# Feed-forward hidden tiles of a hybrid layer made in seven block products in place of eight, with halved weights and weight sums on GpSimd

## The chip, the core and the metric

One core of a Trainium2 chip runs the whole program. The time is device microseconds of one execution of that core. The five engines work beside each other, each through its own instructions in order: TensorE (PE, with its weight loads PEld), VectorE (DVE), ScalarE (ACT), GpSimd (POOL) and SyncE (SP, which here only issues transfers). They wait for each other by semaphores.

## What is computed

One layer over 1056 tokens (1024 of a prompt, 32 of a second group) of 1024 features, in float32. `c` gives nine modulation rows; each of three steps is modulated, gated and normed:

```python
mod = (silu(c) @ w_ada + b_ada)                # 9 rows of 1024, for each of two groups
f = swiglu(modulate(x, 0), w1, w3, w2)         # silu(h @ w1) * (h @ w3), then @ w2; 2816 hidden
x = layer_norm(ALPHA * x + 0.5 * gate(0) * f)
m = mix(modulate(x, 1))                        # gated linear recurrence and spatial gating
x = layer_norm(ALPHA * x + gate(1) * m)
f = swiglu(modulate(x, 2), ...)                # second feed-forward, own weights
x = layer_norm(ALPHA * x + 0.5 * gate(2) * f)
```

The change concerns `h @ w1` and `h @ w3` of both feed-forwards.

## The kernel before

**Layout.** Activations lie feature-major: a feature tile of 128 rows by the tokens, in three chunks of 384, 384 and 288 tokens (`CH`). A hidden tile is 128 of the 2816 hidden features; there are 22 in each feed-forward.

**Products.** Float32 numbers are kept as two parts of fp32r, a high and a low one (`split`, line 176: ScalarE copies the high part at L177, VectorE subtracts it from the source at L178, GpSimd does so in a few places of the start and the mixing). A product is three passes, high x high, high x low and low x high (`h_mm`, all through `mm`, L132). Each matmul has one weight load of its own.

**A hidden tile** (`H`, from L639): for w1 and then w3, eight contraction tiles by three chunks by three passes, into three PSUM banks. ScalarE makes silu of the first (L659), VectorE multiplies it with the second out of PSUM (L666), and the result is split into `g`. The banks come from eight that everything shares.

**An F pass** (`F`, from L745) multiplies the hidden tiles of a block with their w2, for eight output tiles m and three chunks; `add_gated` (L713) adds gate x product to the running sum `xa` (first feed-forward) or `xb` (second). Blocks are nine pairs, [18] and [19, 20, 21]; `ffn_order` lets one further hidden tile run ahead of each pass. The first three hidden tiles are made in special loops (`ffn_first`, `H_chunks`), the last block in `last_f`, chunk by chunk with the norm behind it.

**Weights** come in 512 KB raw tiles (four buffers, by SP's transfers `raw<-wst`) in the order of `stream_order`, and are split into five buffers `whl` of 128 x 2 x 1024. `w_rel` splits the next as one is used up.

**The modulation.** Rows 0 and 1 are made at the start on TensorE. Rows 2 to 8 are made beside the first feed-forward in `ada_rest` (from L576): each in two halves of 512, as 16 products of a raw tile with a number per partition on VectorE (L601, L603, accumulator `acc`), split (`acchl`), summed over partitions by TensorE (`psm`), copied out by ScalarE (L620) to `row`, written to HBM by a GpSimd transfer (L622, `mrow`) and read back turned by two more (L625); VectorE adds the bias (L627, `mod`). Row 2 is the gate `gt` of the first feed-forward, so its first gated addition needs it.

**Order.** TensorE's instructions stand in program order. Those of VectorE, ScalarE and GpSimd are ordered by a scheduler within the program; `ada_rest` is a side program that is taken up as TensorE's work passes by (`yield` gives microseconds of it).

Of the kernel before, what the change touches and what calls it, by code (L numbers as in the profile page):

```python
# [29 lines left out]
# token chunks; the last one ends with the 32 sample tokens  # L30
# [4 lines left out]
# columns of the packed per-feature vectors  # L35
# [10 lines left out]
# row-parallel blocks of the feed-forward's hidden tiles  # L46
BLOCKS = [[2 * b, 2 * b + 1] for b in range(9)] + [[18], [19, 20, 21]]
# [25 lines left out]
def ffn_order():  # L73
    """Program of one feed-forward: ('H', t) and ('F', block), in order."""
    o = [("H", 0), ("H", 1)]
    nxt = 2
    for b in BLOCKS[:-1]:
        o.append(("H", nxt))
        nxt += 1
        o.append(("F", b))  # L80
        if len(b) == 2 and nxt < 19:
            o.append(("H", nxt))
            nxt += 1
    while nxt < FF:
        o.append(("H", nxt))
        nxt += 1
    o.append(("F", BLOCKS[-1]))
    return o


def stream_order():
    s = []
    for n in (1, 2):
        for kind, a in ffn_order():
            if kind == "H":
                s += [(f"f{n}w1", a), (f"f{n}w3", a)]
            else:
                s += [(f"f{n}w2", t) for t in a]
        if n == 1:
            s += [("ga", j) for j in range(4)] + [("xa", j) for j in range(3)]  # L100
            s += [("vs", j) for j in range(4)] + [("xa", 3)] + [("us", j) for j in range(4)]
            s += [("wo", j) for j in range(8)]
    return s


class Tot:
    """A sum over feature tiles: the first `direct` ones go to TensorE alone, VectorE adds the others up in t."""


class Core:  # L110
    def __init__(self, tc, ins, outs):
        self.tc, self.nc = tc, tc.nc
        self.i, self.o = ins, outs
        self.pe = 0.0
        self.side = []
        self.ntot = 2
        self.mods = set()
        self.window = False
        self.ln_out = {}

# [14 lines left out]
    def go(self, gen, kind=None):  # L135
        """Run a side program beside the main one; it yields the time it has to wait."""
# [15 lines left out]
    def drain(self, e, out=False):  # L152
        """Finish a side program, or a norm up to its output; earlier norms first."""
# [7 lines left out]
    def w_init(self):  # L161
        self.order = stream_order()
        self.raws = {}
        self.ws = {}
        self.n_raw = self.n_split = self.n_rel = self.n_get = 0

    def w_raw(self):
        n = self.n_raw
        if n >= len(self.order):
            return  # L170
        r = self.wpool.tile([P, 1024], F32, tag="raw", name="raw", bufs=4)
        self.nc.sync.dma_start(r, self.i["wst"][n])
        self.raws[n] = r
# [5 lines left out]

    def w_split(self, e=None):  # L180
        n = self.n_split
        e = e or (self.nc.gpsimd if self.window else None)
        if n >= len(self.order):
            return
        while self.n_raw <= n:
            self.w_raw()
        w = self.wpool.tile([P, 2, 1024], F32R, tag="whl", name="whl", bufs=5)
        r = self.raws.pop(n)
        self.split(w[:, 0, :], w[:, 1, :], r, e)
# [3 lines left out]
    def w_get(self, what):  # L193
        n = self.n_get
# [14 lines left out]
    def run(self):  # L209
# [4 lines left out]
        # pools over PSUM have eight one-bank buffers  # L214
# [38 lines left out]
        with tc.manual_schedule(engines={E.DVE, E.Activation, E.Pool}):  # L253
# [38 lines left out]
    def startup(self):  # L292
# [29 lines left out]
        # silu(c) in its two parts: [feature, k, (part, group)]  # L322
# [24 lines left out]
        def turn(i):  # L347
            """Rows i, turned, into two banks of four feature tiles."""
# [1002 lines left out]
```

## Time and profile before

| | |
|---|---|
| runs, median of 3 | 1986.9 us (1986.7 to 1988.58) |
| the profiled execution's span | 1981.3 us; 5.6 us of the median lie around it |
| start and the first three hidden tiles | up to 137.9 us |
| first feed-forward, 200 to 600 us | PE busy 400.0 of 400, VectorE 260.2, ScalarE 78.2, GpSimd 20.5 |
| end of the first feed-forward and mixing, 800 to 1200 us | PE busy 387.7 of 400, VectorE 271.1, clock 0.97 |
| second feed-forward, 1200 to 1800 us | PE busy 600.0 of 600, VectorE 227.5, ScalarE 115.3, GpSimd 0.9 |
| DMA | 70 GB/s over the span |

The page gives busy time and share of the span for each engine; a group's row has line, engine, operation, tiles, shapes and count, then the busy time in us and the mean of one in ns, then the idle time just ahead and what ended it. A window's row has start and end, length, and the busy time (with counts) of the engines. A row of the timeline has start, length, engine, line and operation. Waits of the present:

```
engine line waited for: us in total, times, longest us
DVE mod L627 <- DMA mod<-mrow: 26.7, 13, 4.5
POOL mod L625 <- DMA mrow<-row: 45.7, 14, 4.0
ACT g L177 <- DVE s L666: 318.0, 38, 12.5
```

### The profile page before, as it was taken

The numbers are of one execution on the slowest core, as the hardware profiler recorded it, in microseconds if no ns is written. First come the engines' busy times: TensorE is split into PE (matmuls) and PEld (weight loads), VectorE is DVE, ScalarE is ACT, GpSimd is POOL, SyncE is SP. The second block draws the span as 40 slices with busy tenths as digits, with TensorE's granted clock in tenths as the row PEclk, the third lists the DMA queues.
The fourth block names the chain that finished last, engine by engine and source line by source line (L and its number), as shares of the span: only waits on it lengthen the run. The fifth ranks groups of instructions, "written<-read, shape, count | busy, mean of one in ns | idle before, by whom it ended". The sixth has DMA issues, their size and how long they took to land.

```text
span 1981.3 us, 27961 instructions
## 1 busy us (share of the span) xinstructions
PE 1931.3 (97%) x11818; PEld 1886.5 (95%) x11818; DVE 1096.0 (55%) x1988; ACT 540.8 (27%) x848; POOL 90.4 (5%) x102
## 2 busy tenths in 40 slices
PE   7999999999999999989999999999999999999996
PEld 4899999999999999989889999999999999999996
DVE  8885765765664344763977375432442343244457
ACT  6542121212112111244544347111111111111114
POOL 2100000000000000022000000000000000000000
PEclk9999999999999999989899999999999999999998
DMA  7333223222322111121012311111111111110102
GB/s 281 130 126 101 95 84 117 97 75 96 102 95 71 54 43 44 54 80 67 14 59 67 130 36 40 54 43 54 43 34 63 43 43 44 54 43 33 33 1 88
DMA packets 40429, 140.13 MB, mean 71 GB/s; under 512 B 5588, under 2 KB 8276, under 8 KB 39536
## 3 DMA queue, kind: packets, MB, share of 16 engines
q1 hardware_dynamic: 37040, 128.98, 18.8%
q10 hardware_dynamic: 1920, 9.24, 1.2%
q0 software_dynamic: 1344, 0.12, 0.4%
q8 instruction: 93, 1.52, 0.3%
q14 instruction: 32, 0.26, 0.0%
HBM read 129.53 MB, written 8.79 MB: 70 GB/s over the span
## 4 chain that ended last, share of the span: by engine, by line
PE 78%; issue 10%; DVE 7%; ACT 2%; DMA 2%; POOL 0%; SPq 0%; POOLq 0%; DVEq 0%; ACTq 0%
PE ps L132 74%; PE psl L132 1%; DVE xl L462 1%; DVE acc L603 1%; PE psm L132 1%; PE psa L132 1%; DMA mod<-mrow 1%; PE psg L132 1%; DVE tot L719 0%; DMA mrow<-row 0%; ACT t L452 0%; DMA raw<-ada 0%; DVE xa L713 0%; DVE xb L832 0%; DVE t L843 0%
## 5 line engine op out<-in xcount | busy, mean ns | idle before, releaser
L132 PE MATMUL ps<-xh,whl 128*128 128x384 f32 (+1 forms) x5184 | 1245.4, 324 | 2.4 <-ACT xh L459 1.9
L132 PEld LDWEIGHTS ps<-xh,whl 128*128 128x128 f32 x5184 | 910.5, 189 | 7.0 <-ACT xh L459 2.1
L132 PE MATMUL ps<-xl,whl 128*128 128x384 f32 (+1 forms) x2592 | 839.3, 324 | 4.2 <-DVE xl L462 4.2
L132 PE MATMUL ps<-g,whl 128*128 128x384 f32 (+1 forms) x3168 | 522.2, 325 | 1.8 <-DVE xa L713 1.3
L132 PEld LDWEIGHTS ps<-g,whl 128*128 128x128 f32 x3168 | 513.2, 189 | 6.8 <-DVE xa L713 1.9
L132 PEld LDWEIGHTS ps<-xl,whl 128*128 128x128 f32 x2592 | 488.2, 188 | 7.7 <-DVE xl L462 6.0
L178 DVE TENSOR_TENSOR whl<-raw,whl 128x1024 fp32r<-128x1024 f32 x145 | 176.9, 1232 | 265.2 <-ACT whl L177 265.1
L177 ACT ACTIVATE whl<-raw 128x1024 fp32r<-128x1024 f32 x156 | 164.3, 1056 | 361.0 <-PE ps L132 356.6
L713 DVE SCALAR_TENSOR_TENSOR xb<-ps,gt,xb 128x384 f32<-128x384 f32 (+2 forms) x384 | 165.2, 486 | 109.6 <-PE ps L132 95.3
L666 DVE TENSOR_TENSOR s<-s,ps 128x384 f32<-128x384 f32 (+1 forms) x117 | 56.1, 520 | 246.9 <-PE ps L132 246.9
L603 DVE SCALAR_TENSOR_TENSOR acc<-raw,cs,acc 128x512 f32<-128x512 f32 x196 | 137.4, 747 | 56.9 <-DMA raw<-ada 56.9
L713 DVE SCALAR_TENSOR_TENSOR xa<-ps,gt,xa 128x256 f32<-128x256 f32 (+1 forms) x352 | 149.6, 487 | 17.1 <-PE ps L132 16.7
L177 ACT ACTIVATE g<-s 128x384 fp32r<-128x384 f32 x132 | 60.6, 488 | 342.7 <-DVE s L666 318.0
L659 ACT ACTIVATE s<-ps 128x384 f32<-128x384 f32 (+1 forms) x114 | 51.1, 457 | 277.2 <-PE ps L132 276.6
L178 DVE TENSOR_TENSOR g<-s,g 128x384 fp32r<-128x384 f32 x132 | 65.2, 519 | 3.8 <-ACT g L177 3.8
L476 POOL TENSOR_TENSOR r<-r,half 128x3 f32<-128x3 f32 x8 | 7.4, 920 | 1143.2 <-DVE r L475 1143.2
L462 DVE TENSOR_TENSOR xl<-t,xh 128x384 fp32r<-128x384 f32 (+3 forms) x48 | 42.4, 886 | 17.2 <-ACT xh L459 16.4
L132 PE MATMUL ps<-whl,xh 128*128 128x512 f32 (+1 forms) x144 | 46.4, 404 | 0.0
L177 ACT ACTIVATE acchl<-acc 128x512 fp32r<-128x512 f32 x28 | 17.7, 633 | 97.4 <-DVE acc L603 88.6
L452 ACT ACTIVATE t<-xa,AB 128x384 f32<-128x384 f32 (+1 forms) x64 | 34.1, 596 | 34.6 <-DVE AB L506 20.0
L132 PEld LDWEIGHTS ps<-whl,xh 128*128 128x128 f32 (+1 forms) x144 | 26.6, 187 | 7.1
L470 ACT ACTIVATE xb<-xb,aB,aG 128x384 f32<-128x384 f32 (+1 forms) x48 | 28.6, 669 | 14.3 <-DMA xb<-sp 14.3
(188 smaller groups left out, 899.8 us busy)
## 6 DMA issues: line engine op xcount, KB each, us to landing
raw<-wst SPq DMA_DIRECT2D x156, 512.0 KB, 3.2
raw<-ada SPq DMA_DIRECT2D x64, 512.0 KB, 3.3
wnat<-ada SPq DMA_DIRECT2D x4, 1024.0 KB, 13.0
xt<-x SPq DMA_DIRECT2D x7, 512.0 KB, 7.4
sp<-xa ACTq DMA_DIRECT2D x2, 1536.0 KB, 5.1
xb<-sp ACTq DMA_DIRECT2D x2, 1536.0 KB, 10.2
y<-xb SPq DMA_DIRECT2D x4, 768.0 KB, 3.2
sp<-xa ACTq DMA_DIRECT2D x1, 1152.0 KB, 4.1
```

Of the source, the lines that this page charges most:

```text
L132: self.nc.tensor.matmul(out, a, b, start=start, stop=stop, skip_group_check=True)
L177: self.nc.scalar.activation(dst_h, src, AF.Copy)
L178: (e or self.nc.vector).tensor_tensor(dst_l, src, dst_h.bitcast(F32), ALU.subtract)
L452: self.nc.scalar.activation(tmp[:, j, a:a + w], X[:, k, a:a + w], AF.Identity, scale=self.A[:, s, k, v:v + 1], bias=self.B[:, s, k, v:v + 1])
L462: V.tensor_tensor(xl, tmp, xh.bitcast(F32), ALU.subtract)
L470: return self.nc.scalar.activation(X[:, k, :], X[:, k, :], AF.Identity, scale=self.aG[:, s, k:k + 1], bias=self.aB[:, s, k:k + 1])
L476: self.nc.gpsimd.tensor_tensor(out, out, self.half[:n, :w], ALU.pow)
L603: V.scalar_tensor_tensor(acc[:, v, :], r[:, kk, :], self.cs[:, k, v:v + 1], acc[:, v, :], ALU.mult, ALU.add)
L659: self.nc.scalar.activation(s[:, :n], ps[c][:, :n], AF.Silu)
L666: self.nc.vector.tensor_tensor(s, s, ps[c][:, :n], ALU.mult)
L713: V.scalar_tensor_tensor(X[:, m, a + o:a + o + w], ps[:, o:o + w], self.gt[:, s, m, v:v + 1], X[:, m, a + o:a + o + w], ALU.mult, ALU.add)
```

## The change

For hidden tiles 3 to 21 of both feed-forwards (38 of 44), chunks 0 and 1 are computed by the Strassen-Winograd scheme. A tile's weights are seen as a 2 x 2 matrix of blocks: rows w1 and w3, columns the contraction's halves k 0-3 and 4-7 (A11, A12 for w1, A21, A22 for w3). The activations are B11, B21 (halves of chunk 0) and B12, B22 (of chunk 1). Then

S1 = A21 + A22, S2 = S1 - A11, S3 = A11 - A21, S4 = A12 - S2; T1 = B12 - B11, T3 = B22 - B12, T2 = T3 + B11, T4 = B21 - T2.

Seven products A11 B11, A12 B21, S4 B22, A22 T4, S1 T1, S2 T2, S3 T3 and some sums give the four results; eight were needed before. The T are made once in each feed-forward on VectorE (`combs`, `comb_last`; T2 takes B12's place), the S for each tile by four GpSimd sums out of the raw tiles (L238 to L243), and GpSimd also makes the low parts of these four (152). Chunk 2 is made as before, by the halves A11, A12, A21, A22 (`third`).

The core of the diff, the new tile (`H_fast`; `p_mm` is a block product of 4 contraction tiles x 3 passes):

```diff
+        self.p_mm(pa, a11, B11, True, False)
+        S.activation(s1, pa[:, :n], AF.Copy)
+        third(0, 0, a11)
...
+        self.p_mm(pb, s2, self.T2, True, False)
+        add(u2, s1, pb)
...
+        self.p_mm(pa, a12, B21, False, True)
+        sa = self.silu(0, pa)
+        third(0, 1, a12)
...
+        self.p_mm(pc, w, self.T1, True, False)
...
+        self.p_mm(pb, w, self.T3, False, True)
+        add(s1, s1, pb)
+        add(u4, s1, pc)
...
+        self.p_mm(pf, a22, self.T4, True, True)
+        add(s1, s1, pf)
+        self.glu_end(g, 0, sa, s1)
...
+        self.p_mm(pc, w, B22, False, True)
+        add(u2, u2, pc)
+        S.activation(u2, u2, AF.Silu)
+        self.glu_end(g, 1, u2, u4)
```

`add` is a VectorE sum out of PSUM (L838), `glu_end` the multiplication (L679) and the split. The sums of the weights:

```diff
+        if h == "S2":
+            x = self.wpool.tile([P, 1024], F32, tag="raw", name="wsum", bufs=RAWS)
+            G.tensor_tensor(x[:, 0:512], a["A21"], a["A22"], ALU.add)
+            G.tensor_tensor(x[:, 512:1024], x[:, 0:512], a["A11"], ALU.subtract)
+        if h == "S3":
+            G.tensor_tensor(a["A11"], a["A11"], a["A21"], ALU.subtract)
+        if h == "S4":
+            G.tensor_tensor(a["A12"], a["A12"], self.sums[nm, t][:, 512:1024], ALU.subtract)
```

Around it:

- Weights are split in halves of 512 columns into a ring of eight buffers `wh` of 128 x 2 x 512 (five of 1024 before), with a few homes elsewhere; there are five raw buffers (four before), which also hold the S.
- Blocks are [0, 1, 2], then pairs [3, 4] to [17, 18], then [19, 20, 21]; a block's F pass follows its last hidden tile directly, in two halves of w2.
- In `ada_rest` the accumulator has one buffer (two before), the split halves have a place of their own, and a half row goes out as two pieces of 256, by two transfers (L733), before the two that read it back (L736); the bias is added at L738, and the products are L715 and L717.
- The last tile's chunk 2 is made later, between products of its F pass.
- The start's natural weights come in 512 KB pieces; GpSimd's space for descriptors is 1024 bytes.

**Three places in the engines' orders.** First, VectorE in the modulation phase, near the seventh hidden tile. Before (waits for a semaphore in brackets; DMASW is a GpSimd transfer, DMAHW one of SP, names end in a running number):

```order
L666 TENSOR_TENSOR s_1012<-s_1012,ps_1018 128x384 [waits PE_49]
L603 SCALAR_TENSOR_TENSOR acc_1093<-raw_1094,cs_80,acc_1093 128x512 [waits DMAHW6_49,DVE_49]
L603 SCALAR_TENSOR_TENSOR acc_1093<-raw_1094,cs_80,acc_1093 128x512 [waits DVE_49] x3
L178 TENSOR_TENSOR whl_1136<-raw_882,whl_1136 128x1024 [waits DMAHW7_49,Activation_49]
L627 TENSOR_TENSOR mod_74<-mod_74,vec_68 128x8 [waits DMASW2_49,DMASW1_49]
L178 TENSOR_TENSOR g_901<-s_1012,g_901 128x384 [waits Activation_49]
L666 TENSOR_TENSOR s_1014<-s_1014,ps_1019 128x384
L666 TENSOR_TENSOR s_1016<-s_1016,ps_1020 128x288
L603 SCALAR_TENSOR_TENSOR acc_1093<-raw_1115,cs_80,acc_1093 128x512 [waits DMAHW7_49,DVE_49]
L178 TENSOR_TENSOR g_901<-s_1014,g_901 128x384 [waits Activation_49]
L178 TENSOR_TENSOR g_901<-s_1016,g_901 128x288 [waits Activation_49]
```

After:

```order
L738 TENSOR_TENSOR mod_74<-mod_74,vec_68 128x8 [waits DMASW7_49,DMASW6_49]
L717 SCALAR_TENSOR_TENSOR acc_3297<-raw_3368,cs_80,acc_3297 128x512 [waits DMAHW7_49,DVE_49]
L528 SCALAR_TENSOR_TENSOR AB_75<-mod_74,vec_68 128x16 [waits DVE_49]
L529 SCALAR_TENSOR_TENSOR AB_75<-mod_74,vec_68 128x16
L838 TENSOR_TENSOR s_3222<-s_3222,ps_3207 128x384 [waits PE_49]
L530 TENSOR_TENSOR AB_75<-AB_75,mod_74 128x16 [waits DVE_49]
L717 SCALAR_TENSOR_TENSOR acc_3297<-raw_3368,cs_80,acc_3297 128x512
L838 TENSOR_TENSOR s_3354<-s_3222,ps_3208 128x384 [waits DMASW5_49,DVE_49]
L717 SCALAR_TENSOR_TENSOR acc_3297<-raw_3368,cs_80,acc_3297 128x512
L838 TENSOR_TENSOR s_3222<-s_3222,ps_3209 128x384 [waits DVE_49,PE_49]
L717 SCALAR_TENSOR_TENSOR acc_3297<-raw_3368,cs_80,acc_3297 128x512
```

The bias addition to `mod`, which waits for two GpSimd transfers, now stands ahead of the block sums L838 of a tile (s1, u4, s1) with modulation products between them; before, it stood ahead of a split and two multiplications of a tile that was complete in PSUM.

Second, GpSimd at a half row of the modulation. Before, only the transfers:

```order
L622 DMA mrow4_1_2791<-row_2789 2x512 [waits DMASW7_49,Activation_49]
L625 DMA mod_74<-mrow4_1_2791 128x4x1 [waits DMASW7_49,DMASW0_49]
L625 DMA mod_74<-mrow4_1_2791 128x4x1
L622 DMA mrow5_0_3161<-row_3159 2x512 [waits DMASW2_49,Activation_49]
L625 DMA mod_74<-mrow5_0_3161 128x4x1 [waits DMASW3_49,DMASW2_49]
L625 DMA mod_74<-mrow5_0_3161 128x4x1
```

After:

```order
L238 TENSOR_TENSOR wsum_3262<-raw_3204 128x512 [waits DMAHW4_49,Pool_49]
L239 TENSOR_TENSOR wsum_3262<-wsum_3262,raw_3095 128x512 [waits DMAHW3_49,Pool_49]
L241 TENSOR_TENSOR raw_3095<-raw_3095,raw_3204 128x512 [waits DMAHW0_49,DVE_49,Pool_49]
L208 TENSOR_TENSOR wh_3261<-wsum_3262,wh_3261 128x512 [waits Activation_49]
L733 DMA mrow4_1_3282<-s_3283 2x256 [waits Activation_49]
L733 DMA mrow4_1_3282<-s_3286 2x256 [waits Activation_49]
L736 DMA mod_74<-mrow4_1_3282 128x4x1 [waits DMASW6_49,DMASW5_49,DMASW4_49]
L736 DMA mod_74<-mrow4_1_3282 128x4x1 [waits DMASW7_49]
L243 TENSOR_TENSOR raw_3095<-raw_3095,wsum_3262 128x512 [waits DVE_49]
L208 TENSOR_TENSOR wh_3338<-wsum_3262,wh_3338 128x512 [waits Activation_49]
```

The row's transfers now stand between sums and low parts of weights, and the sum S4 (L243) and the low parts behind them come after the wait for the first transfers.

Third, VectorE in the second feed-forward, from the end of one F pass into the next hidden tile. Before:

```order
L178 TENSOR_TENSOR whl_14011<-raw_13797,whl_14011 128x1024 [waits DMAHW3_49,Activation_49]
L178 TENSOR_TENSOR whl_14094<-raw_14014,whl_14094 128x1024 [waits DMAHW4_49,Activation_49]
L666 TENSOR_TENSOR s_14099<-s_14099,ps_14105 128x384 [waits PE_49]
L666 TENSOR_TENSOR s_14101<-s_14101,ps_14106 128x384 [waits DVE_49,PE_49]
L666 TENSOR_TENSOR s_14103<-s_14103,ps_14107 128x288 [waits PE_49,Activation_49]
L178 TENSOR_TENSOR g_14018<-s_14099,g_14018 128x384 [waits Activation_49]
L178 TENSOR_TENSOR whl_14180<-raw_14016,whl_14180 128x1024 [waits DMAHW5_49,Activation_49]
L178 TENSOR_TENSOR g_14018<-s_14101,g_14018 128x384 [waits Activation_49]
L178 TENSOR_TENSOR g_14018<-s_14103,g_14018 128x288 [waits Activation_49]
```

After, the second tile of a pair:

```order
L208 TENSOR_TENSOR wh_14203<-raw_14068,wh_14203 128x512 [waits Activation_49]
L838 TENSOR_TENSOR s_14121<-s_14121,ps_14106 128x384 [waits DVE_49,PE_49]
L208 TENSOR_TENSOR wh_14221<-raw_14139,wh_14221 128x512 [waits DMAHW6_49,Activation_49]
L838 TENSOR_TENSOR s_14219<-s_14121,ps_14107 128x384 [waits DVE_49]
L838 TENSOR_TENSOR s_14121<-s_14121,ps_14108 128x384 [waits DVE_49,PE_49]
L679 TENSOR_TENSOR s_14172<-s_14172,s_14121 128x384 [waits DVE_49]
L208 TENSOR_TENSOR g_14236<-s_14172,g_14236 128x384 [waits Activation_49]
L838 TENSOR_TENSOR s_14155<-s_14155,ps_14107 128x384 [waits PE_49]
L679 TENSOR_TENSOR s_14155<-s_14155,s_14219 128x384 [waits Activation_49]
L208 TENSOR_TENSOR wh_14292<-raw_14139,wh_14292 128x512 [waits Activation_49]
L208 TENSOR_TENSOR g_14236<-s_14155,g_14236 128x384 [waits Activation_49]
L679 TENSOR_TENSOR s_14186<-s_14186,ps_14264 128x288 [waits PE_49]
```

A tile's row of three multiplications became sums s1, u4, s1, a multiplication, the sum u2 and two more multiplications, each with its own wait, and a low part of a weight half (the tile `wh` ahead of u4) stands between the first two.

More of the change, by code (lines that the diff above doesn't have):

```diff
@@ L162, in w_init, with home @@
         self.order = stream_order()
+        self.raw_list = raw_order()
         self.raws = {}
         self.ws = {}
+        self.sums = {}
         self.n_raw = self.n_split = self.n_rel = self.n_get = 0
+        self.ring = [self.home(e) is None for e in self.order]
+    def home(self, e):
+        if e[:2] in (("xa", 0), ("xa", 3)):
+            return "mixr", "wx"
+        if e[:2] == ("f2w1", 2):
+            return "gpool", "tx"
+        if e[0] in ("f1w2", "f2w2") and e[1] in BLOCKS[-1] and e[2] == 1:
+            return "gpool", "tx"
+        return None
     def w_raw(self):
         n = self.n_raw
-        if n >= len(self.order):
+        if n >= len(self.raw_list):
             return
-        r = self.wpool.tile([P, 1024], F32, tag="raw", name="raw", bufs=4)
+        r = self.wpool.tile([P, 1024], F32, tag="raw", name="raw", bufs=RAWS)
         self.nc.sync.dma_start(r, self.i["wst"][n])
-        self.raws[n] = r
+        self.raws[self.raw_list[n]] = r
         self.n_raw += 1
@@ L180, in w_split @@
     def w_split(self, e=None):
         n = self.n_split
-        e = e or (self.nc.gpsimd if self.window else None)
         if n >= len(self.order):
             return
-        while self.n_raw <= n:
+        it = self.order[n]
+        e = e or (self.nc.gpsimd if self.window or str(it[2])[0] == "S" else None)
+        while not all(r in self.raws for r in raws_of(it)):
             self.w_raw()
-        w = self.wpool.tile([P, 2, 1024], F32R, tag="whl", name="whl", bufs=5)
-        r = self.raws.pop(n)
@@ L193, in w_get @@
     def w_get(self, what):
+        if len(what) == 2:
+            return [self.w_get((*what, h)) for h in range(2)]
         n = self.n_get
@@ L605, in ada_rest @@
                     yield 2.5 if m == 2 else 7.0
-                hl = []
-                for v in range(2):
-                    if v:
-                        t = self.wpool.tile([P, 2, 512], F32R, tag="raw", name="acchl", bufs=4)
-                    else:
-                        t = self.apool.tile([P, 2, 512], F32R, tag="t4", name="acchl", bufs=2)
-                    self.split(t[:, 0, :], t[:, 1, :], acc[:, v, :])
-                    hl.append(t)
                 yield 5.0 if m == 2 else 9.0
@@ L640, in H @@
         half = t in self.gs
-        if not half:
-            self.gs[t] = self.gpool.tile([P, 2, T], F32R, tag="g", name="g", bufs=3)
-        g = self.gs[t]
-        pss = []
-        for q in range(2):
-            if q == 0 and half:
-                continue
+        ss = self.halves if half else []
+        for q in range(half, 2):
             w = self.w_get((f"f{nf}w{(1, 3)[q]}", t))
@@ new lines, in p_mm, with block @@
+    def p_mm(self, ps, w, x, first, last):
+        xh, xl = x
+        n = xh.shape[2]
+        for k in range(4):
+            wh, wl = w[:, 0, k * P:(k + 1) * P], w[:, 1, k * P:(k + 1) * P]
+            self.mm(ps[:, :n], wh, xh[:, k, :], first and k == 0, False)
+            self.mm(ps[:, :n], wh, xl[:, k, :], False, False)
+            self.mm(ps[:, :n], wl, xh[:, k, :], False, last and k == 3)
+            self.poll()
+    def block(self, i, c):
+        return self.xh[c][:, 4 * i:4 * i + 4, :], self.xl[c][:, 4 * i:4 * i + 4, :]
@@ new lines, in comb, with tx_tile, combs @@
+    def comb(self, dst, op, x, y, k, e):
+        t, u = self.new_s(), self.new_s()
+        for r, i in ((t, 0), (u, 1)):
+            e.tensor_tensor(r, x[i][:, k, :].bitcast(F32), y[i][:, k, :].bitcast(F32), op)
+        e.tensor_tensor(t, t, u, ALU.add)
+        self.split(dst[0][:, k, :], dst[1][:, k, :], t)
+    def tx_tile(self):
+        t = self.gpool.tile([P, 2, 4, 384], F32R, tag="tx", name="tx", bufs=2)
+        return t[:, 0], t[:, 1]
+    def combs(self):
+        V = self.nc.vector
+        B11, B12, B22 = self.block(0, 0), self.block(0, 1), self.block(1, 1)
+        yield 2.0
+        self.T1 = self.tx_tile()
+        for k in range(4):
+            self.comb(self.T1, ALU.subtract, B12, B11, k, V)
+            yield 2.5
+        self.T3 = self.tx_tile()
+        for k in range(4):
+            self.comb(self.T3, ALU.subtract, B22, B12, k, V)
+            yield 2.5
+        while not self.b12_free:
+            yield 1.0
+        self.T2 = B12
+        for k in range(4):
+            self.comb(self.T2, ALU.add, self.T3, B11, k, V)
+            yield 3.0
```

389 lines of the change are left out of this document (258 added, 131 removed).

## The prediction

> **What bounds the kernel now.** I read the share of busy time first, then the chain of waits, then the chain's pieces in order of time.
>
> ```profile
> span 1981.3 us, 27961 instructions
> PE 1931.3 (97%) x11818; PEld 1886.5 (95%) x11818; DVE 1096.0 (55%) x1988; ACT 540.8 (27%) x848; POOL 90.4 (5%) x102
> PE 78%; issue 10%; DVE 7%; ACT 2%; DMA 2%; POOL 0%; SPq 0%; POOLq 0%; DVEq 0%; ACTq 0%
> 137.89 24.43 PE ps L132 x150
> 1210.99 709.76 PE ps L132 x4401
> ```
>
> The columns of the last two are start, length, what. TensorE (PE) is busy 97%; from 137.89 us on the first feed-forward is one piece of products after the other, and the second is a single piece of 709.76 us. So a product less is time less, if the other engines keep up. How fast products go is read from two stretches in which only one shape runs (a mean of one matmul in the profile is its latency, not its pace):
>
> ```profile
> 1194.33:1200.57 6.24, 6.24 (x38) 6.24 (x38) 5.58 (x8) 6.24 (x11) 0.00 (x0) 1.00 0.00 0
> 1225.01:1231.01 6.00, 6.00 (x47) 6.00 (x46) 2.12 (x3) 4.15 (x8) 0.00 (x0) 1.00 0.21 72
> ```
>
> Behind the length stand PE, weight load, DVE, ACT and POOL busy. The first holds 36 matmuls of 384 columns (38 touch its edges): 6.24/36 = 0.173 us each. The second holds 45 of 288: 0.133 us. The clock is 1.00 in both.
>
> **What is removed.** Each of the 38 tiles loses one block product of 4 contraction tiles x 3 passes = 12 matmuls of 384 columns; the order of PE's rows has 456 fewer of them and as many of every other shape. 456 x 0.173 = **79 us**. A block product lasts 2.08 us, chunk 2's share 1.6 us, a whole tile 21.0 us where it lasted 23.1, a pair of tiles with its F pass 65.2 us where it lasted 69.5. The 79 us are on the path throughout. They come half in each feed-forward, 39.5 and 39.5.
>
> The Trainium skill, "TensorE: Matmul & The Clock Gate", section "Back-to-back issue gap", gives N/2.4 + 2.5 ns for an isolated matmul, 162.5 ns at 384 columns; by it the removal would be 74 us. The trace has 173, and 173 stands.
>
> **What is added on VectorE (DVE).**
>
> ```profile
> L178 DVE TENSOR_TENSOR whl<-raw,whl 128x1024 fp32r<-128x1024 f32 x145 | 176.9, 1232 | 265.2 <-ACT whl L177 265.1
> L603 DVE SCALAR_TENSOR_TENSOR acc<-raw,cs,acc 128x512 f32<-128x512 f32 x196 | 137.4, 747 | 56.9 <-DMA raw<-ada 56.9
> L713 DVE SCALAR_TENSOR_TENSOR xa<-ps,gt,xa 128x384 f32<-128x384 f32 x176 | 101.3, 613 | 17.1 <-PE ps L132 16.7
> L178 DVE TENSOR_TENSOR g<-s,g 128x384 fp32r<-128x384 f32 x88 | 48.6, 553 | 3.8 <-ACT g L177 3.8
> L666 DVE TENSOR_TENSOR s<-s,ps 128x384 f32<-128x384 f32 x78 | 41.6, 554 | 246.9 <-PE ps L132 246.9
> L178 DVE TENSOR_TENSOR acchl<-acc,acchl 128x512 fp32r<-128x512 f32 x28 | 19.1, 690 | 3.1 <-ACT acchl L177 2.3
> L666 DVE TENSOR_TENSOR s<-s,ps 128x288 f32<-128x288 f32 x39 | 17.6, 452 | 0.0
> L132 PE MATMUL ps<-g,whl 128*128 128x384 f32 (+1 forms) x3168 | 522.2, 325 | 1.8 <-DVE xa L713 1.3
> 1497.00:1566.50 69.50, 26.14 (x50) 1.00 0.14 46
> 200.00:300.00 100.00, 100.00 (x617) 98.27 (x616) 70.29 (x136) 19.69 (x31) 6.14 (x9) 1.00 0.28 90
> ```
>
> The row from 1497.00 is one pair of the second feed-forward: VectorE works 26.1 us of 69.5. Of a fast tile, five block sums, two multiplications (each 0.554) and one of 288 columns (0.45) replace three multiplications: +2.8 us, 5.6 a pair. The low parts go from six of 1.23 us a pair to twelve halves of 0.69 (the row acchl has that width; four more a tile are on GpSimd): 8.3 for 7.4. So about 32.7 us of 65.2: half idle, hidden. In the first feed-forward the 200-300 row has 70.29%, 48.9 us in the time of a pair; with +6.5 it is about **55 of 65.2, 85%**, before any wait. That cover is thin. ScalarE (ACT, 540.8 us or 27%) makes the high parts in halves and 38 copies of s1: hidden.
>
> **What is added on GpSimd (POOL).** 152 sums and 152 low parts of 512, 16 operations a pair. None of that width stands in the trace; the nearest rows are the 1024 wide ones:
>
> ```profile
> 905.10 2.40 POOL L178 TENSOR_TENSOR whl<-raw,whl 128x1024 fp32r<-128x1024 f32 x1 [20.27 <-ACT whl L177]
> 846.25 0.46 DVE L719 TENSOR_TENSOR tot<-tot,xa 128x288 f32<-128x288 f32 x1
> 846.62 0.96 DVE L843 TENSOR_TENSOR t<-t 128x768 f32<-128x768 f32 x1
> 847.28 9.46 POOL L178 TENSOR_TENSOR whl<-raw,whl 128x1024 fp32r<-128x1024 f32 x3 [18.25 <-ACT whl L177]
> 849.38 2.10 DVE L719 TENSOR_TENSOR tot<-tot,xa 128x288 f32<-128x288 f32 x1
> 851.40 0.63 DVE L713 SCALAR_TENSOR_TENSOR xa<-ps,gt,xa 128x32 f32<-128x32 f32 x2
> 851.95 2.59 DVE L843 TENSOR_TENSOR t<-t 128x768 f32<-128x768 f32 x1
> 854.47 2.59 DVE L719 TENSOR_TENSOR tot<-tot,xa 128x288 f32<-128x288 f32 x1
> ```
>
> Half of 2.40 is 1.2, with a fixed part at most 2.40; I take 1.3 (21 us a pair, a third of GpSimd's time). The dearer part is beside it: while GpSimd ran 9.46 us, the sum L719, 0.46 us alone, took 2.10 and 2.59, while those that read PSUM (851.40) passed in their usual time. Two-input VectorE work out of SBUF and GpSimd exclude each other here; L719 twice and L843 (0.96 just before) lost 1.64 + 2.13 + 1.63 = 5.4 us of 9.46, 57%. So 16 x 1.3 us cost VectorE between 0 (it was idle) and 20.8 us a pair (all lost), at 57% 12. In the second feed-forward 33 + 12 of 65.2 is hidden. In the first, 55 + 12 = 67 is the pair's whole time.
>
> The Trainium skill, "GPSIMD Engine Reference", section "4.1 Engine selection", says that elementwise work belongs on VectorE, and "SBUF — State Buffer", section "SBUF: two separate sides", that the two hold their port as an exclusive lock, the loser fully blocked; the 2.59 rows agree with the second. By the first the sums would stand on VectorE: 16 x 0.69 = 11 us a pair, no better than the lock at 57%.
>
> **What waits newly.** The block sums stand in VectorE's line in program order with the modulation's work, and each is due within one block product: u4 must have read its bank before S4 writes into it, 2.08 us after S3's product ends, with s1's sum ahead of it (0.55 + 0.55). Before, a late L666 cost nothing for a whole product (it waited 246.9 us for PE, PE not for it). Now a modulation row's end stands in that place:
>
> ```profile
> 460.20 0.54 POOL L622 DMA_DIRECT2D mrow<-row  x1 [35.91 <-ACT row L620]
> 464.61 1.51 POOL L625 DMA_DIRECT2D mod<-mrow  x2 [3.87 <-DMA mrow<-row]
> 467.98 0.17 DVE L627 TENSOR_TENSOR mod<-mod,vec 128x8 f32<-128x8 f32 x1 [2.32 <-DMA mod<-mrow]
> ```
>
> From the row's first DMA to the addition of b_ada lie 7.8 us; after the change there are two row DMAs (+0.5) and GpSimd sums in between (1.3 or more). VectorE stands at that addition (L738) with block sums queued behind it, and TensorE for them. It falls inside a fast tile in some five of the fourteen half rows (tiles 6, 7, 10, 14, 15), 1.5 to 4.4 us each by the order, **14 us**; small misses of the 2.08 us at each of 13 more tiles in this phase (four modulation products of 0.75, L603 before, L717 now, queued between s1 and u4) 0.3 to 0.5, **6 us**. An F pass now follows its last hidden tile at once: before, a whole tile lay between. TensorE's products with g stood 1.8 us in all then (the row PE ps<-g above). Chunk 2 of that tile is now due 21 matmuls, 3.4 us, after its products end, with a multiplication, an ACT copy and a low part to go, and the raw buffers serve sums too; the modulation already waits for its own raws (56.9 us above, unfelt). I take 1 us for each of 8 passes, **8 us**. In the second feed-forward none of the modulation is there: only one low part of 0.69 stands between s1 and u4 in every second tile, 0.55 + 0.69 + 0.55 of 2.08: **5 us** (2 to 12).
>
> **The start.**
>
> ```profile
> 83.00:137.90 54.90, 53.59 (x330) 52.04 (x328) 44.52 (x76) 27.99 (x51) 4.32 (x6) 1.00 0.49 162
> 132.82 1.38 DVE L666 TENSOR_TENSOR s<-s,ps 128x384 f32<-128x384 f32 x3
> ```
>
> Here VectorE is at 81%. T1, T3 and T2 (12 combinations, each two sums and an addition of 0.55 and a low part, 2.2 us: 26 us) come into this stretch and the next tiles, in front of gt and the first gated additions. Added up row by row in the new order, VectorE comes to the multiplications of tile 2 some 51 us after 83 us, no later than before (132.8). But the column sums of modulation row 2, which stand in TensorE's own order, wait for an accumulator that stands behind the combinations, about 7 and 4 us, and a bank of PSUM comes free 2 us late: **13 us** (8 to 18). Mixing, where halves replace whole weights, and the tail, where tile 21's chunk 2 is made late to cover the additions: 2 us (-3 to 7).
>
> **The sum.** -79 + 13 + 14 + 6 + 8 + 5 + 2 = **-31 us**. Against this execution: 1981.3 - 31 = 1950 us of span; the median of the runs, 1986.9, is 5.6 more, so **1956 us**. The first feed-forward then gains nothing (39.5 against 41), the second about 35. With the unknown terms low (start 8, first feed-forward 8, second 2, rest -3) it is -64: 1923; with them high (18, its 28 twice over, 12, 7) +14: 2001.
>
> **Rivals.**
> 1. The cover holds. The scheduler put sums early enough, the lock falls in VectorE's idle time, raws are on time. For it: 85% is not 100%, PE hardly waits for VectorE now. Against: the 2.08 us and the 7.8 us row. It keeps the start and a few us more, -55 to -64: about **1927**. 0.18.
> 2. The first feed-forward gives back more than it gained: lock at 57% puts VectorE at 67 of 65.2 us and the waits for rows come on top, since there is no idle time to catch up in: (67 - 65.2) x 8 pairs = 14 us beyond my sum and a few more at the rows, -13: **1974** (1970 to 1983). 0.21.
> 3. Slower. One mechanism: the exclusion of VectorE by GpSimd in the modulation phase. With all of 20.8 us lost, VectorE needs 76 of 65.2 us, 10.6 x 8 pairs = 85 us; with start 13, second 5, rest 2 and the rows' 14 that is -79 + 119 = +40: **2027**. It decides from an overrun of about 5.6 us a pair, that is at three quarters of GpSimd's time lost, or at 57% with 1.7 us an operation. For it: the rows from 851.95 lose 3.76 of 5.1 us, just that; against: those are back to back on both sides, and half of VectorE's work here reads PSUM and passes. 0.14.
> 4. The change does not do what it says: PE's pace follows the weight loads, and fewer products bring less. Against: every matmul removed takes its load along, and 36 of them stood at 0.173 with PE full. 0.02; at half the gain per matmul it would give 1995.
>
> **How the numbers follow.** My forecast, -16 to -50, gets 0.45; rival 1 0.18; rival 2 0.21; rival 3 0.14; rival 4 0.02. The range leaves out the far part of rival 3 and little of rival 1: **1922 to 1998**. Differences of 0.2% (4 us) are about what a measurement of this kernel can tell. Faster by more: 0.45 + 0.18 + 0.18 = 0.81 (some of rival 2 ends near nothing); within: 0.04; slower: 0.15 (rival 3, half of rival 4).
>
> **What will show it.** In the profile after, 456 matmuls fewer; in the second feed-forward the chain should again be nearly one piece, with pairs of 65 to 66 us. VectorE's waits for GpSimd's DMA (mod<-mrow) should exceed the 26 us of before, and the chain should name DVE and mod<-mrow between 140 and 640 us. VectorE should be 85 to 95% busy between 200 and 600 us; at 99% rival 2 or 3 holds, at 80% with PE full rival 1. GpSimd's operations of 512 should take 1.2 to 1.6 us alone, and as long as a VectorE operation more where they meet. I am wrong if PE stands in the second feed-forward for more than 12 us, or if the first gains more than 20.

## The result, and the profile after

Slower, a little: 2001.24 us (1999.37 to 2003.04) against 1987.74 us (1986.7 to 1989.89), four runs each; ratio 1.0064, interval 1.005 to 1.0078. The forecast of 1956 us and its range were missed. The page of the kernel after, span, busy times and chain of waits (followed back from the end, this chain reaches only to 765 us, so its shares say nothing of the first feed-forward):

```profile
span 2000.3 us, 28452 instructions
PE 1876.9 (94%) x11362; PEld 1819.9 (91%) x11362; DVE 1346.2 (67%) x2390; ACT 709.2 (35%) x1240; POOL 524.8 (26%) x428
PE 54%; DVE 5%; ACT 1%; issue 0%; POOL 0%; DMA 0%; POOLq 0%; DVEq 0%; ACTq 0%
```

The 456 matmuls are gone, yet the span grew by 19 us. Where it went shows when the program is cut at the same places in both kernels: from the first F product of a feed-forward to the first column sum of its norm (from, to, length, then PE, weight load, DVE, ACT and POOL busy, granted clock). Before, first and second feed-forward:

```profile
129.57:812.98 683.41, 682.10 (x4190) 673.50 (x4189) 399.87 (x770) 126.02 (x207) 25.62 (x37) 1.00 0.24 80
1250.47:1920.58 670.11, 670.11 (x4142) 669.13 (x4141) 263.64 (x509) 104.24 (x171) 0.00 (x0) 1.00 0.12 42
```

After:

```profile
152.30:877.12 724.82, 666.52 (x3962) 651.37 (x3961) 525.75 (x923) 201.60 (x380) 248.91 (x200) 0.96 0.24 77
1311.06:1940.88 629.82, 628.61 (x3914) 626.69 (x3913) 356.78 (x662) 184.30 (x332) 200.72 (x150) 1.00 0.13 45
```

The second feed-forward is 40.3 us shorter. The first is 41.4 us longer with 228 matmuls fewer, at a mean clock of 0.96, and its first F product comes 22.7 us later (152.30 for 129.57). Mixing and tail are 5 us shorter together: 22.7 + 41.4 - 40.3 - 5 = 19.

From the time between the starts of two matmuls in the trace I subtracted the pace of the prediction (0.173 us for 384 columns, 0.133 for 288). What is left is called a **gap** where it is over 0.4 us, and **half clock** where the clock granted there was under 0.9. For each run (the e's are the experiments below; e9 changes the kernel before and is told in its place):

| kernel | first F product at, us | first feed-forward, us | gaps in it | half clock in it | all that follows it |
|---|---|---|---|---|---|
| before | 129.6 | 683.4 | 1.5 | 0.0 | 1168 |
| after | 152.3 | 724.8 | 61.5 | 22.4 | 1123 |
| e1 no row wait | 154.7 | 686.6 | 36.8 | 9.6 | 1124 |
| e2 late addition | 148.8 | 702.7 | 46.3 | 16.1 | 1123 |
| e3 sums on VectorE | 150.2 | 713.3 | 54.5 | 17.9 | 1124 |
| e4 fast from 17 | 137.5 | 708.2 | 26.8 | 11.1 | 1123 |
| e5 only row 2 | 154.1 | 629.9 | 1.9 | 0.0 | 1124 |
| e6 row buffer | 155.5 | 705.2 | 47.5 | 17.1 | 1122 |
| e7 = e2 + e6 | 153.0 | 680.3 | 29.9 | 9.9 | 1123 |
| e8 = e7, fast from 5 | 138.6 | 697.0 | 40.0 | 12.5 | 1123 |
| e10 = e7 + e3 | 154.2 | 669.3 | 22.5 | 4.8 | 1126 |
| e11 = e7 + e4 | 135.9 | 686.8 | 12.7 | 4.4 | 1124 |
| e12 = e7, T on GpSimd | 159.0 | 678.2 | 27.2 | 10.6 | 1122 |
| e13 = e10 + e4 | 135.6 | 681.7 | 8.8 | 3.1 | 1123 |
| e14 = e10, fast from 9 | 135.7 | 679.1 | 19.5 | 6.7 | 1123 |

One of the gaps, in the timeline of the kernel after (start, length, engine, what, idle time ahead and what ended it):

```profile
300.89 1.06 POOL L733 DMA_DIRECT2D mrow<-s  x2 [7.95 <-ACT s L732]
305.53 0.78 POOL L736 DMA_DIRECT2D mod<-mrow  x1 [3.58 <-issue]
306.79 2.27 PE L149 MATMUL ps<-T,wh 128*128 128x384 f32 x12
308.51 0.78 POOL L736 DMA_DIRECT2D mod<-mrow  x1 [2.20 <-issue]
309.30 1.27 POOL L238 TENSOR_TENSOR wsum<-raw 128x512 f32<-128x512 f32 x1
311.26 0.68 DVE L738 TENSOR_TENSOR mod<-mod,vec 128x8 f32<-128x8 f32 x1 [4.45 <-DMA mod<-mrow]
312.52 0.54 DVE L838 TENSOR_TENSOR s<-s,ps 128x384 f32<-128x384 f32 x1
313.59 0.54 DVE L838 TENSOR_TENSOR s<-s,ps 128x384 f32<-128x384 f32 x1
314.19 0.68 PE L149 MATMUL ps<-xh,wh 128*128 128x384 f32 x1 [5.13 <-DVE s L838]
314.66 0.53 PE L149 MATMUL ps<-xl,wh 128*128 128x384 f32 x1
314.98 0.53 PE L149 MATMUL ps<-xh,wh 128*128 128x384 f32 x1
```

VectorE stands 4.45 us at the bias addition; the sums s1 and u4 (L838) are queued behind it; TensorE has finished A22 T4 (the row from 306.79) and stands 5.13 us until u4 has read the bank into which S4's product goes. Then its matmuls start 0.32 us apart (314.66 and 314.98), where 0.173 is usual: half clock. The chain of one half row was 7.8 us before; here it is 10.4 (300.89 to 311.26). VectorE stands like this at every one of the fourteen half rows (waits in us in total, times, longest), where it stood 26.7 us in thirteen waits before:

```profile
DVE mod L738 <- DMA mod<-mrow: 53.4, 14, 4.9
```

### The profile page after: what moved, and what is told of

It is laid out like the page before. It is cut to its first block, busy times and chain, and to the rows that moved or that the text cites. A ratio compares the mean times of both kernels' runs of the same rounds, so it can differ in the third digit from the quotient of the medians.

```text
span 2000.3 us, 28452 instructions
## 1 busy us (share of the span) xinstructions
PE 1876.9 (94%) x11362; PEld 1819.9 (91%) x11362; DVE 1346.2 (67%) x2390; ACT 709.2 (35%) x1240; POOL 524.8 (26%) x428
## 4 chain that ended last, share of the span: by engine, by line
PE 54%; DVE 5%; ACT 1%; issue 0%; POOL 0%; DMA 0%; POOLq 0%; DVEq 0%; ACTq 0%
PE ps L149 52%; PE psl L149 1%; PE psz L149 1%; DVE s L789 1%; PE psg L149 0%; DVE tot L952 0%; DVE xb L1065 0%; ACT t L543 0%; DVE t L1076 0%; DVE wh L208 0%; DVE xa L946 0%; DVE tx L208 0%; DVE xb L946 0%; ACT xh L550 0%; DVE s L790 0%
## 5 line engine op out<-in xcount | busy, mean ns | idle before, releaser
L149 PE MATMUL ps<-xh,wh 128*128 128x384 f32 (+1 forms) x3824 | 923.0, 324 | 45.1 <-DVE s L838 41.0
L149 PEld LDWEIGHTS ps<-xh,wh 128*128 128x128 f32 x3824 | 677.4, 192 | 55.6 <-DVE s L838 46.5
L149 PE MATMUL ps<-xl,wh 128*128 128x384 f32 (+1 forms) x1912 | 616.9, 323 | 3.3 <-DVE xl L553 3.2
L149 PE MATMUL ps<-g,wh 128*128 128x384 f32 (+1 forms) x2808 | 466.1, 325 | 13.0 <-DVE xa L946 4.7
L149 PEld LDWEIGHTS ps<-g,wh 128*128 128x128 f32 x2808 | 453.6, 189 | 19.6 <-DVE xa L946 6.7
L207 ACT ACTIVATE wh<-raw 128x512 fp32r<-128x512 f32 x376 | 234.7, 629 | 540.5 <-PE ps L149 517.1
L149 PEld LDWEIGHTS ps<-xl,wh 128*128 128x128 f32 x1912 | 367.4, 192 | 7.3 <-DVE xl L553 5.3
L208 DVE TENSOR_TENSOR wh<-raw,wh 128x512 fp32r<-128x512 f32 x283 | 207.2, 737 | 197.8 <-ACT wh L207 195.6
L717 DVE SCALAR_TENSOR_TENSOR acc<-raw,cs,acc 128x512 f32<-128x512 f32 x196 | 168.8, 897 | 6.5 <-DMA raw<-ada 6.3
L149 PE MATMUL ps<-tx,wh 128*128 128x384 f32 x912 | 167.3, 338 | 2.7 <-DVE s L838 2.6
L838 DVE TENSOR_TENSOR s<-s,ps 128x384 f32<-128x384 f32 x190 | 104.7, 551 | 87.4 <-PE ps L149 79.7
L149 PEld LDWEIGHTS ps<-tx,wh 128*128 128x128 f32 x912 | 158.9, 190 | 4.4 <-DVE s L838 3.6
L238 POOL TENSOR_TENSOR wsum<-raw 128x512 f32<-128x512 f32 x38 | 57.8, 1522 | 142.4 <-DVE wh L208 86.0
```

Of the source, the lines that this page charges most:

```text
L149: self.nc.tensor.matmul(out, a, b, start=start, stop=stop, skip_group_check=True)
L207: self.nc.scalar.activation(dst_h, src, AF.Copy)
L208: (e or self.nc.vector).tensor_tensor(dst_l, src, dst_h.bitcast(F32), ALU.subtract)
L238: G.tensor_tensor(x[:, 0:512], a["A21"], a["A22"], ALU.add)
L717: V.scalar_tensor_tensor(acc[:, v, :], r[:, kk, :], self.cs[:, k, v:v + 1], acc[:, v, :], ALU.mult, ALU.add)
L838: V.tensor_tensor(out, x, ps[:, :n], ALU.add)
```

## The experiments

**e1 to e4: the wait, the exclusion, or the amount of work?** Theory A is the gap just shown. Theory B is my third rival, VectorE too full under GpSimd's exclusion.

e1 lets the transfers write rows 3 to 8 where nobody reads them, and sets the rows to zero at the start (so the kernel's result is another):

```diff
-    nc.gpsimd.dma_start(self.mod[:, m, 4 * h:4 * h + 4, v], ...)
+    nc.gpsimd.dma_start(self.mod[:, m if m == 2 else m % 2, 4 * h:4 * h + 4, v], ...)
```

> The kernel after, but the GpSimd transfers that read modulation rows 3 to 8 back write where nobody reads, and the rows stay zero plus their bias (so gates, scales and shifts of the later steps are other numbers); the transfers are still issued. Theory A (VectorE stands at the bias addition L738 for those transfers with a tile's block sums queued behind it, TensorE then stands for S4's product, and each such stall is followed by a stretch of half clock): of TensorE's gaps of 2.4 to 8.7 us between 170 and 800 us the eight that follow a wait for mod<-mrow go, about 41 us, and some 15 us of half clock with them: 1945 us (1935 to 1960). Theory B (my rival 3: VectorE with the exclusion by GpSimd is simply too full in the modulation phase): nothing is removed from VectorE but 53 us of standing that would refill with queued work: 1990 to 2001.

Measured 1970.08 us, ratio to before 0.9915 (0.99 to 0.993): 31 us less than after. This lies between the ranges of the two theories. Gaps and half clock fall by 25 and 13 us, as the first theory has it, but half of them stay.

e2 puts `V.tensor_tensor(mod, ...)` and what follows from it into a function that runs after the next half row's last products:

```diff
+                    if q == 3 and pend:
+                        pend.pop()()
```

> The kernel after, with each bias addition of rows 3 to 8 (and the coefficients after it) written one half row later, behind the last products of the next half row; all else as it is. Theory A: the transfers have landed where VectorE meets the addition in most of the eleven places, the stalls at those go: 1950 us (1940 to 1970). Theory B: 1995 to 2003, since VectorE's work is the same.

1977.45 us, 0.9956 (0.9942 to 0.9971): 24 of e1's 31 us, the right direction, though it misses theory A's range. VectorE's waits for `mod<-mrow` fall from 53.4 us to this:

```profile
DVE mod L743 <- DMA mod<-mrow: 19.2, 6, 5.2
```

Two of the six are row 2's, which was not moved; at the other four VectorE still came to the addition before its transfer had landed.

e3 sets `G = self.nc.vector` for the four sums and lets VectorE make their low parts.

> The kernel after, with the four weight sums and the low parts of the sums on VectorE, none on GpSimd (304 operations of 0.69 us, 210 us more VectorE work, no exclusion). Theory A: the row waits stay (GpSimd's chain gets about 2 us shorter), VectorE is fuller by 17%: slower, 2005 to 2040. Theory B: if GpSimd's exclusion were what costs the time, VectorE gets back more than it gives: 1970 to 1995.

1989.92 us, 1.002 (1.0002 to 1.0038), ten runs from 1983.94 to 1997.73: 11 us **faster** than after, though VectorE has 304 more operations. Theory A's expectation was wrong here; the time lies in theory B's range. What GpSimd costs shows in VectorE's own durations (mean ns behind the busy time), after and then e3:

```profile
L717 DVE SCALAR_TENSOR_TENSOR acc<-raw,cs,acc 128x512 f32<-128x512 f32 x196 | 168.8, 897 | 6.5 <-DMA raw<-ada 6.3
L679 DVE TENSOR_TENSOR s<-s 128x384 f32<-128x384 f32 x76 | 54.8, 721 | 8.3 <-ACT s L876 7.2
L838 DVE TENSOR_TENSOR s<-s,ps 128x384 f32<-128x384 f32 x190 | 104.7, 551 | 87.4 <-PE ps L149 79.7 <-DMA mrow<-s 6.0
```

```profile
L717 DVE SCALAR_TENSOR_TENSOR acc<-raw,cs,acc 128x512 f32<-128x512 f32 x196 | 138.6, 746 | 5.2 <-DMA raw<-ada 5.1
L679 DVE TENSOR_TENSOR s<-s 128x384 f32<-128x384 f32 x76 | 42.2, 556 | 1.2
L838 DVE TENSOR_TENSOR s<-s,ps 128x384 f32<-128x384 f32 x190 | 104.7, 551 | 46.3 <-PE ps L149 38.1 <-DMA mrow<-s 7.3
```

The operations L717 and L679, with two inputs in SBUF, are 20 and 30% longer beside GpSimd; the block sums, which read PSUM, are the same 551 ns. Added up over the operations that both kernels have, VectorE lost 66 us in the first feed-forward and 27 in the second. So the exclusion is there, and theory B has part of the cause. It is not the main part: without any weight sum on GpSimd 72 of the 84 us of gaps and half clock stay (54.5 and 17.9 in the table). VectorE was not full on average either, 471 of 630 us between 170 and 800 us in the kernel after; that it was full for short stretches is not excluded by this.

e4 is `FAST = {1: range(17, FF), ...}` with the T made two blocks earlier than tile 17.

> The kernel after, with hidden tiles 3 to 16 of the first feed-forward made the old way (eight block products, in the new halves) and only tiles 17 to 21 fast, the combinations T made just before them; second feed-forward as after. Theory A: a normal tile has no sum that is due within 2 us, so the row waits cost nothing as before the change; the start has no combinations in front of row 2: 1987 - 39.5 - 5 x 2.08 + some 3 at the switch: 1940 us (1933 to 1952). Theory B: also faster, since tiles 3 to 16 bring no VectorE work, but F passes directly behind their tile and halved weights, if these were what costs, would leave 1955 to 1975.

1974.17 us, 0.9943 (0.9926 to 0.9959), 34 us above theory A's figure and in theory B's range. The start is right (137.5), but the first feed-forward, normal tiles for the most part, still has 38 us of gaps and half clock: TensorE's waits are now for the most part at F passes, which stand directly behind their tile. Whether these feel the same standing VectorE or cost by themselves is settled by e5 and e11.

**e5 to e8: which part of the modulation.** The L838 row above names a second wait, `DMA mrow<-s`: the half row's two pieces stand in `s` buffers, and a tile's u4 takes such a buffer only when the row's transfer has read it.

e5 is `for m in (2,):`, with the coefficients made from zero rows.

> The kernel after without modulation rows 3 to 8 (their loads, products, column sums and transfers are left out, the rows stay zero, so later gates, scales and shifts are other numbers); row 2 and all of the feed-forward as after. Theory A (VectorE's queue is held up by the modulation, and each stall of TensorE brings half clock): the gaps of 61.5 and the slow stretches of 22.4 us in the first feed-forward go to under 8 together, as in the second, the start keeps its 22 us: 1922 us (1912 to 1934). Theory C (the fast tiles themselves, F passes directly behind their tile, the raw buffers, GpSimd's exclusion): 20 to 40 of the 84 us stay: 1940 to 1965.

1906.53 us, 0.9588 (0.956 to 0.9617), below even A's range; the modulation's own column sums are left out too, and in the kernel before, the first feed-forward, which alone has them, was 11.8 us longer than the second without its gaps (683.4 - 1.5 - 670.1):

```profile
154.10:784.01 629.91, 628.35 (x3914) 625.88 (x3913) 359.74 (x695) 184.77 (x332) 203.21 (x152) 1.00 0.15 49
```

Fast tiles, F passes and GpSimd's sums are all there, and the first feed-forward is as long as the second, at a clock of 1.00. Theory C is out: without modulation rows 3 to 8 only 1.9 of the 84 us are left. But e5 takes the modulation's work (VectorE busy 359.74 us here, 525.75 after) together with its waits, so it doesn't say which of the two it was. The start is as late as in the kernel after (154.10).

e6 gives the half row a buffer of its own and one transfer, as before the change:

```diff
-                for q in range(2):
-                    row = self.new_s()[0:2, 0:256]
...
+                row = self.apool.tile([P, 512], F32, tag="tot", name="row", bufs=self.ntot)[0:2]
+                nc.scalar.activation(row, ps[0:2, :], AF.Copy)
+                nc.gpsimd.dma_start(d, row)
```

> The kernel after with one thing undone: a modulation half row leaves PSUM in one piece, in a buffer of the kind that holds its split halves, and by one transfer, as before the change, in place of two pieces in the s buffers of the hidden tiles. No u4 and no multiplication then waits for a row's transfer, and the read-back is two transfers in one go. Theory A': part of the row's price is not the addition but the s buffers and a chain that is 2 to 3 us longer: 15 us of gaps and 5 of half clock go: 1982 us (1974 to 1992). If only the addition counts: 1993 to 2003, the chain being a little shorter.

1983.9 us, 0.9987 (0.9974 to 0.9999): 17 us, as expected of A'. The half row shown above, in e6:

```profile
299.44 0.55 POOL L732 DMA_DIRECT2D mrow<-row  x1 [8.14 <-ACT row L731]
307.00 0.78 DVE L737 TENSOR_TENSOR mod<-mod,vec 128x8 f32<-128x8 f32 x1 [1.97 <-DMA mod<-mrow]
310.03 0.45 PE L149 MATMUL ps<-xh,wh 128*128 128x384 f32 x1 [2.64 <-DVE s L837]
```

Its chain is 7.6 us where it was 10.4, and TensorE stands 2.64 us where it stood 5.13. So the 17 us are the shorter chain and the freed `s` buffers together; no run separates them. The waits that name `DMA mrow<-s` in the L838 row are 6.0 us.

> e6's and e2's edits together. Theory A': both waits are gone, and it beats each of them and e1 (which kept the s buffers): 1960 us (1950 to 1969). If the addition alone counts: e2's 1977 (1972 to 1982).

1957.11 us, 0.9853 (0.9833 to 0.9873): 44 us less than after, about the sum of both (24 and 17). A' holds. Of the 84 us of gaps and half clock 40 stay.

> e7's edits, and in the first feed-forward tiles 3 and 4 made the old way, so that the combinations T stand behind modulation row 2 and not in front of it. The start's extra gaps and half clock (16 + 10 us) go but for a few, two tiles of 2.1 us are lost, and there may be a stall of some 6 us where the fast tiles begin (e4 had one): 1948 us (1938 to 1960). If the combinations only move their stall: 1958 to 1966.

1961.3 us, 0.9868 (0.9846 to 0.9891). The start got its time back (138.6), the first feed-forward lost it again (697.0 for 680.3): the stall moved with the combinations.

**e9: what a stall costs.** Behind hidden tiles 4 to 15 of the second feed-forward of the kernel before:

```diff
+            S.activation(x[:, :288], ps[2][:, :288], AF.Copy)
+            for i in range(t - 4):
+                S.activation(x[:, :288], x[:, :288].bitcast(F32), AF.Copy)
+            self.mm(pl[0:2, :288], self.one_r[:, 0, :], x[:, :288], True, True)
```

> The kernel before, with one stall of TensorE put behind each of the hidden tiles 4 to 15 of the second feed-forward: a tiny matmul of two columns whose input is copied out of the tile's last bank by ScalarE and then copied onto itself 0, 1, 2 ... 11 times (about 0.45 us a copy), so the stalls grow from under 1 us to some 6 us. Nothing of the kernel's result depends on it. Theory H (a stall costs its length and, beyond some length between 1.7 and 2.4 us, a stretch of half clock behind it, as the gaps of the kernel after suggest): no half clock behind the first two or three, 3.4 us of it behind the next, 6.8 or more behind stalls over 5 us; total 44 us of stalls and some 15 to 20 of half clock: about 2045 us. Rival: half clock comes from something else in the first feed-forward (such as GpSimd's or VectorE's load), and these stalls cost their length alone: about 2030 us and a clock of 1.00.

One run, 2061.46 us against 1986.47. The tiny matmul at four rungs, with TensorE's idle time ahead of it:

```profile
1324.92 0.29 PE L132 MATMUL psd<-lad,one_r 128*2 128x288 f32 x1 [1.52 <-ACT lad L666]
1373.86 0.30 PE L132 MATMUL psd<-lad,one_r 128*2 128x288 f32 x1 [2.27 <-ACT lad L668]
1481.60 0.40 PE L132 MATMUL psd<-lad,one_r 128*2 128x288 f32 x1 [3.69 <-ACT lad L668]
1791.78 0.40 PE L132 MATMUL psd<-lad,one_r 128*2 128x288 f32 x1 [7.20 <-ACT lad L668]
```

The 10 us behind each (the clock is the first number after the five engines):

```profile
1325.00:1335.00 10.00, 10.00 (x63) 10.00 (x63) 7.11 (x16) 0.73 (x2) 0.00 (x0) 1.00 0.16 52
1374.00:1384.00 10.00, 10.00 (x53) 10.00 (x53) 1.31 (x4) 0.44 (x1) 0.00 (x0) 0.83 0.16 52
1482.00:1492.00 10.00, 10.00 (x49) 10.00 (x49) 3.89 (x9) 0.00 (x0) 0.00 (x0) 0.76 0.09 37
1792.00:1802.00 10.00, 10.00 (x48) 10.00 (x48) 0.00 (x0) 0.00 (x0) 0.00 (x0) 0.73 0.01 2
```

A clock of 0.83 over 10 us is 3.4 us at half, that of 1.00 none. A stall of 1.52 us leaves the clock alone; all eleven from 2.27 us on come with half clock that costs 1.3 to 2.7 us more, with little regard to their length: behind the longer ones the half clock begins while TensorE still stands (the longest stall ends at 1791.78, its half clock began at 1787.19). Stalls of 56 us in all and some 20 of half clock make the 75 us. Theory H holds, as a rule and not to the tenth: elsewhere a stall of 2.41 us (the kernel after, at 165.88) and one of 2.82 us (e1, at 212.48) were not followed by it, and one of 2.07 us (e4, at 373.93) was. The Trainium skill, "TensorE: Matmul & The Clock Gate", section "What's actually happening", has the clock halved after an idle window of about 3.4 us that runs free of the kernel. The trace's half-clock stretches are multiples of 3.41 us, but a stall of 2.27 us was enough. Where they differ, the measurement decides.

**e10 to e14: what is left, and a version that beats both.**

> e7 with the weights' sums and their low parts on VectorE (e3's edit), none on GpSimd. If GpSimd's exclusion is what is left in the first feed-forward (30 us of gaps, 10 of half clock): 1945 us (1940 to 1952), as e3 was 11 us faster than the kernel after. If what is left is VectorE's queue itself (modulation products and raw waits ahead of a tile's sums): VectorE has 17% more to do there: 1957 to 1980.

1948.69 us, 0.9805 (0.9786 to 0.9824): 8 us less than e7, what moving the sums off GpSimd is worth here, with VectorE's added work already paid.

> e7 with tiles 3 to 16 of the first feed-forward made the old way (e4's edit). If e4's 27 us of gaps and 11 of half clock were the same two waits, felt where an F pass stands directly behind its tile, they go but for some 10 us, and the start keeps e4's 126 us: 1941 us (1934 to 1952). If they come from the F passes alone: 1957 to 1966.

1948.27 us, 0.981 (0.9796 to 0.9825), 7 us above the expectation: the two waits were e4's loss for the most part (38 us of gaps and half clock became 17).

> e7 with the sums of T1 and T3 of the first feed-forward on GpSimd (24 operations of 384 columns, 13 us less on VectorE; low parts stay). If the start's 24 extra us are VectorE's amount of work in front of modulation row 2: 10 us less: 1947 us (1942 to 1954). If GpSimd's exclusion gives it back: 1955 to 1965.

1958.68 us, 0.9864 (0.9842 to 0.9885): nothing gained, as expected for the case that the exclusion gives it back; the first F product comes later (159.0).

> e10 (row in its own buffer, addition late, sums on VectorE) with tiles 3 to 16 of the first feed-forward made the old way. If what is left is VectorE's amount of work under the modulation: FFN1's gaps and half clock fall from e11's 17 us to under 12, since the five fast tiles run without GpSimd: 1944 us (1938 to 1949). If the stall is at the place where fast tiles begin: 1946 to 1952, as e11.

1941.66 us, 0.9779 (0.9761 to 0.9798), in the range for VectorE's amount of work and outside that for the place where the fast tiles begin: less overlap, 11.9 us of gaps and half clock.

> e10 with tiles 3 to 8 made the old way. The start loses its 18 us against e10 (combinations behind row 2), six tiles of 2.1 us are lost (12.5), and of e10's 27 us of gaps and half clock the part of the tiles before 9 goes (some 7), while 5 to 8 may come where the fast tiles begin: 1940 us (1933 to 1950), the fastest of all. If the combinations press as hard in the middle of the modulation as at the start: 1950 to 1960.

1937.94 us, 0.9761 (0.9743 to 0.9779): the fastest, 49 us under before and 63 under after.

## Why the prediction was wrong, point by point

- **What bounds it, and the 79 us: right.** The second feed-forward, with 228 matmuls fewer, became 40.3 us shorter (39.5 said). Its small terms were too dear: 5 us said for late sums, 1.4 us of gaps found.
- **VectorE's and GpSimd's amounts: right.** A sum on GpSimd takes 1.27 us (1.3 said); VectorE is 57% busy in the second feed-forward (356.8 of 629.8) where 50% was said. Its 525.8 us in the first are 83% of the 629.9 us that e5 takes there without stalls, where 85% was said; with the stalls it is only 75% between 170 and 800 us.
- **The exclusion: mechanism right, size too large.** Taken as 12 us of VectorE's time a pair, it is about 7 in the first feed-forward and 3 in the second (the 66 and 27 us of e3 over 9.5 pairs); to the kernel it is worth 8 to 11 us (e3, e10). Rival 3 was the one with the right sign, but its cause is the smaller part of the loss.
- **The step that failed is "What waits newly".** It priced the addition at 14 us in five places, small misses at 6, F passes at 8: 28 us. The table has 84 us, and all but 1.9 of them need modulation rows 3 to 8 (e5). The length of the chain was about right (7.8 + 0.5 + 1.3 or more was said, 10.4 found). What was wrong: VectorE stands at the addition in all fourteen half rows, 2.8 to 4.9 us each, where five were priced; making the addition late brings 24 us (e2). The row's pieces in the `s` buffers and the longer chain of two transfers were not priced as stalls of their own, though the order shows u4 waiting for a GpSimd transfer (DMASW5); undoing both brings 17 us (e6), with the late addition 44 (e7). And **the sum had no term for the clock**: there are 22 us of half clock in the first feed-forward, and in e9 every stall from 2.27 us on brought some.
- **F passes: wrong cause.** By themselves they cost next to nothing (e5: 1.9 us of gaps in all), 8 us said; beside the modulation they stand with everything else (e4, e11).
- **The start: 13 us said, 22.7 found.** TensorE stands before the column sums `psm`, as said, for 4.25, 2.77 and 6.18 us where about 7 and 4 were priced, with two stretches of half clock. Most of it goes when the T come later (e4, e8, e11, e13, e14: 135.6 to 138.6).
- **Mixing and tail:** 5 us faster, 2 us slower said.
- Of the signs, the waits for `mod<-mrow` doubled (26.7 to 53.4 us) as said. VectorE's share between 200 and 600 us is 75% (298.3 of 400), under all that the signs named, because it stood waiting; a clock under 1.00 was not among them.

What stays open: in e10 the first feed-forward still has 27 us of gaps and half clock, and e13 only shows that they shrink with the overlap. The late addition still waits there at places (30.6 us for `mod<-mrow` in e10), once for 5.36 us just ahead of a stall of 4.24 us (at 355.00), so that some of the rest is the same wait; how much is not shown. The second read-back transfer also starts some 2.1 us after the first has been issued, in e6 too, where before they went one behind the other; the change left GpSimd less space for descriptors, and whether that is the reason no run shows.

## What to carry to other kernels

When a change turns work that may be late into work that is due within 2 us, look at everything that can **wait** in the same engine's queue, not at its share of busy time: VectorE was three quarters busy, and TensorE still lost 84 us. Give side work's results their own buffers and a short chain, and write the instruction that waits for a transfer where the transfer has long landed. Count a TensorE stall above some 2 us as its length and about 2 us more, which is what e9's ladder came to (20 us behind eleven stalls).

## What the runs showed of the hardware

A stall of TensorE of 1.52 us left the clock at 1.00, one of 2.27 us halved it for 3.41 us; from 3.69 us on it was mostly 6.83, and at 7.20 us 10.24 (e9). Between 2.0 and 2.8 us other kernels show both outcomes. Two kinds of VectorE operations with two SBUF inputs were 20 and 30% longer beside a GpSimd that was busy a third of the time (897 for 746 ns, 721 for 556), the low parts of weight halves only 7% (737 for 692), and the sums that read PSUM not at all (551 and 551). Summing 128 x 512 weights on VectorE was faster for the kernel than on GpSimd, which had little else to do, by 11 us (e3) and 8 us (e10).
